# A state-space layer on Trainium2: scratch and powers of VectorE's complex products in PSUM, another layout for the gated unit's inputs, another order on GpSimd

## The chip, the cores and the metric

The kernel runs on one core of a Trainium2 chip. The metric is the device time of one execution in microseconds (us); times shown are medians over runs. The profile is of one such execution.

## The reference

A two-layer decoder trunk on 512 tokens of width 1024, all in float32. Layer 0 mixes tokens with a diagonal complex state-space model (64 groups of 16 channels, 64 states each), then a gated unit, layer norm and a dense SwiGLU block. Layer 1 is latent attention followed by a routed SwiGLU block with 8 experts, of which each token takes 2. The change touches the state-space mixer and what hands its result to the gated unit:

```python
lb_re = mag * jnp.cos(li * dt)
lb_im = mag * jnp.sin(li * dt)
...
bb_re = f_re[..., None] * br - f_im[..., None] * bi
bb_im = f_re[..., None] * bi + f_im[..., None] * br
...
_, _, s_re, s_im = lax.associative_scan(_s5_combine, (a_re, a_im, bu_re, bu_im), axis=0)
y = (jnp.einsum('sbgp,gcp->bsgc', s_re, c_re.astype(f32))
     - jnp.einsum('sbgp,gcp->bsgc', s_im, c_im.astype(f32)))
y = y.reshape(bsz, seq, D_MODEL) + d_skip.astype(f32) * uf
act = jax.nn.gelu(y).astype(u.dtype)
val, gate = jnp.split(act @ w_glu, 2, axis=-1)
return val * jax.nn.sigmoid(gate)
```

## The kernel before

The 512 tokens are cut into 64 blocks of 8 (j is the block, t the token in it). Within a block the recurrence is worked out as matrices, and only the 64 block states are scanned. The 64 groups lie two to a column of 128 partitions (2 groups x 64 states), so there are 32 columns; they are worked on in two halves of 16. All complex tensors have an axis of two, real and imaginary.

For each half `h` there are:

- **A** (`s5_a`, L1829): the input factors of the 8 tokens of a block, 128 x 2 x 16 x 128, made from `bb` by complex products (`cmul`) with powers of the diagonal (`self.pw`, three powers).
- **O** (`s5_o`, L1913): the output factors, made in the same way from C.
- **E** (`s5_e`, L1768): unit phases of the 64 blocks, always made by GpSimd. With them the scan runs on real decays.
- **the input pass** (`s5_in`, L1840): PE transposes A (L1853), ScalarE copies it out of PSUM (L1854), PE multiplies with the tokens U (L1870), and `turn` (L1876) rotates each block of four columns by E into S. A pass has four such turns.
- **the scan** (`s5_scan`, L1887): two VectorE scans (L1893) and four turns back, SBUF to SBUF.
- **K** (`s5_k`, L1947): PE makes the within-block kernels from O and bz; ScalarE copies them out, and 16 small transfers on SP's queue (for half 1, four of them on GpSimd's) write the block-Toeplitz tile T.
- **y** (`s5_y`, L1979): two calls for each half; PE multiplies T with U and O with S, ScalarE applies the gelu.
- **hand-over** (`s5_act`, L2008): for each y, eight PE transposes into two PSUM banks; ScalarE writes the float16 high part (L2018), VectorE subtracts it from the bank for the low part (L2019). Both are written with the token's position in its block as the slow axis, so that neighbours of one instruction lie 8 elements apart.

`cmul` (L1778) does a complex product in three steps: `tensor_mul` of the swapped parts into a scratch tile (L1792), `tensor_mul` by the real part (L1798), `tensor_add` of the scratch (L1799). For long rows on VectorE the last two are one `scalar_tensor_tensor` per column (L1795). The scratch tile is in SBUF, one for VectorE (`s5_ctv`, shared with `turn`) and one for GpSimd (`s5_ctp`). In `turn` L1881 writes the scratch, L1882 the other product, and L1885 twice adds or subtracts the scratch in place:

```python
V.tensor_mul(t, self.swap(x), E[:, 1, None].to_broadcast(sh))
V.tensor_mul(dst, x, E[:, 0, None].to_broadcast(sh))
for part in range(2):
    op = V.tensor_add if back == (part == 0) else V.tensor_sub
    op(dst[:, part], dst[:, part], t[:, part])
```

**What sets the order.** The program is written out by hand and each engine works through its own instructions in the order in which `run` (L2022) issues them. VectorE makes O and A of half 0; GpSimd makes E of both halves and then A of half 1; VectorE does the turns and scans and O of half 1. After scan 0 come the first chunk of the gated unit's weights (`st.load(1)`, `st.convert(1)`: ScalarE L102, then VectorE L103), 36 matmuls that keep PE busy (`warm`, L270), y of half 0, its hand-over, the input pass, K and scan of half 1. Weight chunks are loaded on SP's queue. PSUM is one pool of 8 banks of 128 x 512 floats for everything (`bank`, L250). `glu_quarter` (L294) then does the gated unit in four quarters of the columns. Its first half quarter needs the hand-over of half 0 alone; y and hand-over of half 1 are issued inside the first quarter. After that come the dense block, attention and the experts.

Of the kernel before, what the change touches and what calls it, by code (L numbers as in the profile page):

```python
# [20 lines left out]
L = 8  # L21
# [102 lines left out]
class Kernel:  # L124
    def __init__(self, tc, A, out, dev=None):
        self.tc, self.nc, self.A, self.out = tc, tc.nc, A, out
        self.dev = dev or {}
        self.pools = []

    def pool(self, name, side, **kw):  # L130
# [119 lines left out]
    def bank(self, name="ps"):  # L250
        return self.ps.tile([128, 512], F, name=name, tag="ps", bufs=8)

# [1398 lines left out]
    def s5_params(self):  # L1651
# [73 lines left out]
        for i in range(3):  # L1725
            if i:
                re, im = P[:, i - 1, 0], P[:, i - 1, 2]
                V.tensor_mul(t[:, 0], re, re)
                V.tensor_mul(t[:, 1], im, im)
                V.tensor_sub(P[:, i, 0], t[:, 0], t[:, 1])  # L1730
                V.scalar_tensor_tensor(P[:, i, 2], re, 2.0, im, op0=OP.mult, op1=OP.mult)
            V.tensor_scalar(P[:, i, 1::2], P[:, i, 2, None, :].to_broadcast([128, 2, 32]), -1.0, None, op0=OP.mult)
        self.bb = self.r3.tile([128, 2, 32, GC], F, name="s5_bb")
        self.cmul(V, self.bb, self.b, f, 0, 32)
# [42 lines left out]

    def cmul(self, eng, dst, x, cf, g0, g1, conj=False):  # L1778


        n = x.shape[3]
        step = min(g1 - g0, 512 // n)
        cr = cf[:, 0, None, :, None]
        ci = cf[:, 2:4] if conj else cf[:, 1:3]
        nm = "s5_ctv" if eng is self.nc.vector else "s5_ctp"
        for g in range(g0, g1, step):
            s = slice(g, g + step)
            sh = [128, 2, step, n]
            t = self.r3.tile([128, 2, 512], F, name=nm, tag=nm, bufs=1)[:, :, :step * n]
            t = t.rearrange("p a (g n) -> p a g n", n=n)  # L1790
            xs = x[:, :, s]
            eng.tensor_mul(t, self.swap(xs), ci[:, :, s, None].to_broadcast(sh))  # L1792
            if n >= 64 and eng is self.nc.vector:
                for i in range(step):
                    eng.scalar_tensor_tensor(dst[:, :, g + i], x[:, :, g + i], cf[:, 0, g + i:g + i + 1], t[:, :, i],  # L1795
                                             op0=OP.mult, op1=OP.add)
                continue
            eng.tensor_mul(dst[:, :, s], xs, cr[:, :, s].to_broadcast(sh))  # L1798
            eng.tensor_add(dst[:, :, s], dst[:, :, s], t)  # L1799
# [29 lines left out]
    def s5_a(self, eng, h):  # L1829
        A = self.wp.tile([128, 2, 16, L * GC], F, name="s5_A", tag="wf", bufs=2)  # L1830
        at = lambda t0, t1: A[:, :, :, t0 * GC:t1 * GC]
        hs = slice(h * 16, h * 16 + 16)
        pw = lambda i: self.pw[:, i, :, hs]
        self.cmul(eng, at(7, 8), self.bb[:, :, hs], pw(0), 0, 16)
        self.cmul(eng, at(6, 7), at(7, 8), pw(0), 0, 16)
        self.cmul(eng, at(4, 6), at(6, 8), pw(1), 0, 16)
        self.cmul(eng, at(0, 4), at(4, 8), pw(2), 0, 16)
        return A
# [74 lines left out]
    def s5_o(self, eng, h):  # L1913
        hs = slice(h * 16, h * 16 + 16)
        ot = lambda l0, l1: self.O[:, :, hs, l0 * GC:l1 * GC]
        for i, n in enumerate((1, 2, 4)):
            self.cmul(eng, ot(n, 2 * n), ot(0, n), self.pw[:, i, :, hs], 0, 16, conj=True)

# [89 lines left out]
    def s5_act(self, dp):  # L2008
        nc = self.nc
        y = self.ydt.pop(dp)  # L2010
        for t0 in (0, 4):
            p = self.bank()
            for t in range(4):
                nc.tensor.transpose(p[:, t * 128:(t + 1) * 128], y[:, t0 + t].rearrange("j i q c -> j (i q c)"), self.ident)
            pv = p.rearrange("p (t r j) -> p r t j", t=4, r=2)
            hi, lo = (x[:, 2 * dp:2 * dp + 2].rearrange("p r (j t) -> p r t j", t=L)[:, :, t0:t0 + 4]
                      for x in (self.xh, self.xl))
# [4 lines left out]
    def run(self):  # L2022
# [7 lines left out]
        self.YD = dram.tile([SEQ, D], F, name="YD")  # L2030
        psA = self.ps = self.pool("psA", None, space=bass.MemoryType.PSUM)
        self.wp = self.pool("w", "right")
        self.big = self.pool("big", "left")
        if phases != "moe":
# [13 lines left out]
            self.s5_u()  # L2048
            E = [self.s5_e(nc.gpsimd, h) for h in range(2)]
            self.s5_o(V, 0)  # L2050
# [16 lines left out]
            st.load(1)  # L2067
            st.convert(1)
            self.warm(36)
            self.s5_y(0)  # L2070
# [4 lines left out]
            self.xh, self.xl = Halves(None, None), Halves(None, None)  # L2075
            self.s5_xt(0)
            self.s5_act(0)
            self.s5_act(1)
            self.s5_in(1, A1, E[1])
            del A1  # L2080
            self.s5_k(1)
            self.bz = None
            self.s5_scan(1, E[1])
            E = self.dec = None
            st.load(2)
            self.r3.release()
# [63 lines left out]
        keep()  # L2150
        psA.release()
        self.hp = self.pool("moe_h", "right")
# [53 lines left out]
```

## Time and profile before

| | |
|---|---|
| median of 3 runs | 1884.29 us (1880.74 to 1885.18) |
| the profiled execution | 1883.41 us, of which the span is 1881.6 us |
| mean granted TensorE clock | 0.963 of full speed |
| busy: PE, VectorE (DVE), ScalarE (ACT), GpSimd (POOL) | 1741.5, 1443.9, 1011.5, 237.3 us |
| HBM read, mean rate over the span | 416.81 MB, 228 GB/s |

How to read it: the span runs from the first to the last instruction of the core, and the times in the rows further down count from its start. PE is the matrix engine, PEld its weight loads, SP the queue that issues most transfers. Busy time is the time in which an engine's instructions run, so a VectorE instruction that is held up while it runs counts as busy. [...] What stands in brackets behind a row is the idle time of that engine just before it and what ended it.

### The profile page before, as it was taken

To read this page: it belongs to the slowest core of one execution; us is meant where nothing else is said; L and a number is where in the kernel's file an instruction comes from. 1 tells how busy PE (TensorE), PEld (TensorE's weight loads), DVE (VectorE), ACT (ScalarE), POOL (GpSimd) and SP (SyncE) were. 2 spreads that over 40 slices of the span, in tenths; PEclk is the share of its full clock that TensorE was granted. 3 is DMA by queue.
4 is the path that set the end of the run, shared out by engine and by line. 5 is a ranking of instruction groups with operands and counts; after the bars stand their busy time and mean duration, and the time that the engine had idled before them with its cause. 6 is when DMAs were issued, how large, how long until landed. Compare 5 with 4: busy or idle time off the path is not lost.

```text
span 1881.6 us, 45134 instructions
## 1 busy us (share of the span) xinstructions
PE 1741.5 (93%) x19567; PEld 1371.7 (73%) x19567; DVE 1443.9 (77%) x2048; ACT 1011.5 (54%) x1091; POOL 237.3 (13%) x232
## 2 busy tenths in 40 slices
PE   6578989999999788979999999999999999999984
PEld 5445455444444555569999999999999899999963
DVE  9995473333324877569999999999999899999987
ACT  4233343223222466257776666666766677766772
POOL 6940010000000100200000022120000100000035
PEclk9679999999999899979999999999999999999997
DMA  4105803433323210189999999999999999999991
GB/s 85 45 23 170 236 26 90 112 93 108 111 92 88 79 46 1 45 294 378 372 339 339 347 340 332 339 347 342 367 355 349 302 361 380 361 373 360 359 375 59
DMA packets 359393, 433.79 MB, mean 231 GB/s; under 512 B 30520, under 2 KB 321424, under 8 KB 359184
## 3 DMA queue, kind: packets, MB, share of 16 engines
q1 hardware_dynamic: 346832, 417.55, 65.7%
q0 software_dynamic: 4064, 12.72, 2.4%
q8 instruction: 155, 2.54, 0.6%
q10 hardware_dynamic: 8288, 0.54, 0.3%
q14 instruction: 54, 0.44, 0.1%
HBM read 416.81 MB, written 11.34 MB: 228 GB/s over the span
## 4 chain that ended last, share of the span: by engine, by line
PE 75%; DVE 15%; ACT 3%; issue 3%; DMA 3%; POOL 1%; DVEq 0%; ACTq 0%; POOLq 0%
PE gu L274 10%; PE gu L276 10%; PE gu L275 10%; PE ps L275 6%; PE ps L276 6%; PE ps L274 6%; PE y L274 5%; PE y L275 5%; PE y L276 5%; DVE wi L1095 2%; PE gu L1043 2%; DMA mraw<-in_moe_w_in_dram 2%; PE glu L276 1%; PE glu L274 1%; PE glu L275 1%
## 5 line engine op out<-in xcount | busy, mean ns | idle before, releaser
L276 PE MATMUL gu<-xe,wi 128*128 128x132 f16 (+7 forms) x3584 | 658.8, 225 | 17.7 <-DVE wi L1095 17.7
L274 PE MATMUL gu<-xe,wi 128*128 128x132 f16 (+7 forms) x3584 | 658.8, 225 | 6.3 <-ACT yr L1180 3.4
L275 PE MATMUL gu<-xe,wi 128*128 128x132 f16 (+7 forms) x3584 | 658.8, 224 | 0.0
L1095 DVE SCALAR_TENSOR_TENSOR wi<-mraw,wi 128x2048 f16<-128x2048 f32 x224 | 511.9, 2285 | 13.5 <-ACT wi L1089 13.5
L1089 ACT ACTIVATE wi<-mraw 128x2048 f16<-128x2048 f32 x224 | 420.8, 1904 | 32.3 <-DMA mraw<-in_moe_w_in_dram 29.5
L276 PEld LDWEIGHTS <-wi 128*128 128x128 f16 x3584 | 352.2, 98 | 19.4 <-DVE wi L1095 19.3
L275 PEld LDWEIGHTS <-wi 128*128 128x128 f16 x3584 | 353.4, 99 | 8.5 <-issue 3.8
L274 PEld LDWEIGHTS <-wi 128*128 128x128 f16 x3584 | 352.5, 98 | 6.7 <-ACT wi L1089 3.0
L1095 DVE SCALAR_TENSOR_TENSOR wol<-mraw,woh 128x2048 f16<-128x2048 f32 x112 | 255.8, 2284 | 0.2 <-ACT woh L1089 0.2
L1089 ACT ACTIVATE woh<-mraw 128x2048 f16<-128x2048 f32 x112 | 213.3, 1904 | 7.3 <-DMA mraw<-in_moe_w_out_dram 7.3
L275 PE MATMUL y<-hl,woh 128*128 128x132 f16 (+4 forms) x1120 | 215.9, 227 | 0.0
L276 PE MATMUL y<-hh,wol 128*128 128x132 f16 (+4 forms) x1120 | 215.9, 227 | 0.0
L274 PE MATMUL y<-hh,woh 128*128 128x132 f16 (+4 forms) x1120 | 215.9, 227 | 0.0
L1112 ACT ACTIVATE hs<-gu 128x168 f32<-128x168 f32 (+5 forms) x224 | 63.5, 284 | 270.1 <-PE gu L276 269.8
L103 DVE SCALAR_TENSOR_TENSOR wf<-raw,wf 128x2048 f16<-128x2048 f32 x37 | 84.9, 2297 | 118.4 <-ACT wf L102 118.4
L1147 POOL DMA_INDIRECT XD<-yr,at x12 | 24.8, 2068 | 807.2 <-ACT yr L1180 442.4
L102 ACT ACTIVATE wf<-raw 128x2048 f16<-128x2048 f32 x37 | 70.5, 1909 | 100.7 <-PE ps L276 67.5
L276 PE MATMUL ps<-xt,wf 128*128 128x512 f16 x320 | 121.3, 379 | 0.0
L275 PE MATMUL ps<-xt,wf 128*128 128x512 f16 x320 | 121.3, 379 | 0.0
L274 PE MATMUL ps<-xt,wf 128*128 128x512 f16 x320 | 121.3, 379 | 0.0
L274 PEld LDWEIGHTS <-woh 128*128 128x128 f16 x1120 | 109.6, 98 | 0.0
L275 PEld LDWEIGHTS <-woh 128*128 128x128 f16 x1120 | 109.6, 98 | 0.1
(462 smaller groups left out, 2888.6 us busy)
## 6 DMA issues: line engine op xcount, KB each, us to landing
mraw<-in_moe_w_in_dram SPq DMA_DIRECT2D x224, 1024.0 KB
mraw<-in_moe_w_out_dram SPq DMA_DIRECT2D x112, 1024.0 KB
raw<-in_ffn_w_in_dram SPq DMA_DIRECT2D x44, 512.0 KB
raw<-in_ffn_w_out_dram SPq DMA_DIRECT2D x11, 1024.0 KB
raw<-in_s_w_glu_dram SPq DMA_DIRECT2D x64, 128.0 KB
raw<-in_mla_o_w_dram SPq DMA_DIRECT2D x4, 1024.0 KB
XD<-X SPq DMA_DIRECT2D x5, 512.0 KB
xj<-in_x_dram SPq DMA_DIRECT2D x4, 512.0 KB
```

Source lines behind the costliest of these rows:

```text
L102: nc.scalar.activation(hi[:, c], raw[:, c], AF.Copy, scale=scale[j])
L103: nc.vector.scalar_tensor_tensor(lo[:, c], raw[:, c], scale[j], hi[:, c], op0=OP.mult, op1=OP.subtract)
L274: mm(out, lh, rh, start=first, stop=False, **kw)
L275: mm(out, lh, rl, start=False, stop=False, **kw)
L276: mm(out, ll, rh, start=False, stop=last, **kw)
L1043: nc.tensor.matmul(p[:, (k - k0) * cap:(k - k0 + 1) * cap], x[:, tt, k * 128:(k + 1) * 128], sel[:, tt, :cap], start=tt == 0, stop=tt == T ...
L1089: nc.scalar.activation(hi, raw, AF.Copy, scale=WS)
L1095: self.nc.vector.scalar_tensor_tensor(lo, raw, WS, hi, op0=OP.mult, op1=OP.subtract)
L1112: nc.scalar.activation(sg, p[:, :cap], AF.Silu, scale=1.0 / (WS * XS))
L1147: self.nc.gpsimd.indirect_dma_start(out=self.XD, out_offset=bass.IndirectOffsetOnAxis(ap=self.at[:n, j:j + 1], axis=0), in_=yr[:n], in_off ...
```

## The change

VectorE's scratch tile moves from SBUF to a PSUM pool of its own (`psT`), for `cmul` and for `turn`. ScalarE copies the powers there too (`pwp`), and VectorE's products take them from it; the per-column scalar of L1795 still comes from SBUF. GpSimd's tiles stay in SBUF. While the state-space stage runs, the pool for everything else has 5 banks instead of 8; after scan 1 both pools are released and the old pool of 8 is opened.

GpSimd makes E of half 0, then A of half 1, then E of half 1. The second `warm` goes. The input pass of half 1 moves ahead of the hand-over of half 0, and the conversion of the first weight chunk moves from before y to behind that pass.

The hand-over writes, for each block, four tokens that lie next to each other. For even pairs (`dp`) it reads the transposes from PSUM with the token as the fastest axis, 128 floats apart; for odd pairs PE writes the transposes with a step of 4 floats, and the reads are in order.

```diff
@@ def bank
-        return self.ps.tile([128, 512], F, name=name, tag="ps", bufs=8)
+        return self.ps.tile([128, 512], F, name=name, tag="ps", bufs=self.nps)
@@ def s5_params
+        self.pwp = self.pt.tile([128, 3, 4, 32], F, name="s5_pwp")
+        nc.scalar.activation(self.pwp, P, AF.Copy)
         self.bb = self.r3.tile([128, 2, 32, GC], F, name="s5_bb")
@@ def power, def cmul
+    def power(self, eng, i, h):
+        return (self.pwp if eng is self.nc.vector else self.pw)[:, i, :, h * 16:h * 16 + 16]
...
-            t = self.r3.tile([128, 2, 512], F, name=nm, tag=nm, bufs=1)[:, :, :step * n]
+            if eng is self.nc.vector:
+                t = self.pt.tile([128, 2, 512], F, name=nm, tag=nm, bufs=1)[:, :, :step * n]
+            else:
+                t = self.r3.tile([128, 2, 512], F, name=nm, tag=nm, bufs=1)[:, :, :step * n]
...
-                    eng.scalar_tensor_tensor(dst[:, :, g + i], x[:, :, g + i], cf[:, 0, g + i:g + i + 1], t[:, :, i],
+                    eng.scalar_tensor_tensor(dst[:, :, g + i], x[:, :, g + i], one[:, 0, g + i:g + i + 1], t[:, :, i],
@@ def s5_a (s5_o likewise)
-        self.cmul(eng, at(0, 4), at(4, 8), pw(2), 0, 16)
+        self.cmul(eng, at(0, 4), at(4, 8), pw(2), 0, 16, one=self.pw[:, 2, :, hs])
@@ def turn
-        t = self.r3.tile([128, 2, 4 * NJ], F, name="s5_ctv", tag="s5_ctv", bufs=1)[:, :, :4 * NJ]
+        t = self.pt.tile([128, 2, 512], F, name="s5_ctv", tag="s5_ctv", bufs=1).rearrange(
+            "p a (i n) -> p (a i n)", n=4 * NJ)[:, :8 * NJ]
@@ def s5_act
+            if dp % 2:
+                pt = p.rearrange("p (r j t) -> p t r j", t=4, r=2)
+                pv = p.rearrange("p (r j t) -> p r j t", t=4, r=2)
+            else:
+                pt = p.rearrange("p (t r j) -> p t r j", t=4, r=2)
+                pv = p.rearrange("p (t r j) -> p r j t", t=4, r=2)
             for t in range(4):
-                nc.tensor.transpose(p[:, t * 128:(t + 1) * 128], y[:, t0 + t].rearrange("j i q c -> j (i q c)"), self.ident)
-            pv = p.rearrange("p (t r j) -> p r t j", t=4, r=2)
-            hi, lo = (x[:, 2 * dp:2 * dp + 2].rearrange("p r (j t) -> p r t j", t=L)[:, :, t0:t0 + 4]
+                nc.tensor.transpose(pt[:, t], y[:, t0 + t].rearrange("j i q c -> j (i q c)"), self.ident)
+            hi, lo = (x[:, 2 * dp:2 * dp + 2].rearrange("p r (j t) -> p r j t", t=L)[:, :, :, t0:t0 + 4]
                       for x in (self.xh, self.xl))
@@ def run
-        psA = self.ps = self.pool("psA", None, space=bass.MemoryType.PSUM)
+            self.ps = self.pool("psS", None, space=bass.MemoryType.PSUM)
+            self.nps = 5
+            self.pt = self.pool("psT", None, space=bass.MemoryType.PSUM)
...
-            E = [self.s5_e(nc.gpsimd, h) for h in range(2)]
+            E = [self.s5_e(nc.gpsimd, 0)]
...
             A1 = self.s5_a(nc.gpsimd, 1)
+            E.append(self.s5_e(nc.gpsimd, 1))
...
             st.load(1)
-            st.convert(1)
-            self.warm(36)
             self.s5_y(0)
             self.s5_o(V, 1)
             self.s5_y(1)
...
             self.s5_xt(0)
+            self.s5_in(1, A1, E[1])
+            del A1
+            st.convert(1)
             self.s5_act(0)
             self.s5_act(1)
-            self.s5_in(1, A1, E[1])
-            del A1
             self.s5_k(1)
             self.bz = None
             self.s5_scan(1, E[1])
             E = self.dec = None
+            self.pt.release()
+            self.ps.release()
+            self.nps = 8
+            self.ps = self.pool("psA", None, space=bass.MemoryType.PSUM)
```

## Rows read from the trace of the kernel before

**Rows 1.** Busy us by stretch: each engine (x instructions), PE clock, DMA share, GB/s.

```profile
62.00:78.00 16.00, 14.34 (x120) 11.23 (x116) 15.48 (x18) 8.05 (x8) 15.21 (x16) 0.92 0.03 11
78.00:112.00 34.00, 16.06 (x120) 9.16 (x120) 33.55 (x21) 1.19 (x2) 31.04 (x15) 0.61 0.04 16
...
260.00:1881.00 1621.00, 1541.81 (x18040) 1248.43 (x18038) 1241.64 (x1732) 920.22 (x988) 133.25 (x112) 0.98 0.74 251
```

**Rows 2.** All runs of two lines: ns min/median/max, first and last start.

```profile
L1881 DVE TENSOR_TENSOR s_ctv<-ps,s_E x8: 682/683/841, 62.4 to 141.9; 128x504 f32<-128x504 f32 x8
L1881 DVE TENSOR_TENSOR s_ctv<-s_S,s_E x8: 682/684/2707, 84.4 to 155.0; 128x504 f32<-128x504 f32 x8
...
L1885 DVE TENSOR_TENSOR s_S<-s_S,s_ctv x32: 414/422/2554, 63.7 to 156.8; 128x252 f32<-128x252 f32 x32
```

**Rows 3.** VectorE in order of time, 0 to 420 us: start us, length us, instructions.

```profile
19.86 1.22 DVE L1792 TENSOR_TENSOR s_ctv<-b,s_f 128x1024 f32<-128x1024 f32 x1
...
46.53 6.62 DVE L1795 SCALAR_TENSOR_TENSOR s_A<-s_A,s_pw,s_ctv 128x128 f32<-128x128 f32 x8
...
56.10 6.14 DVE L1795 SCALAR_TENSOR_TENSOR s_A<-s_A,s_pw,s_ctv 128x128 f32<-128x128 f32 x8
...
78.15 6.19 DVE L1893 TENSOR_TENSOR_SCAN s_S<-dec,s_S 128x1024 f32<-128x1024 f32 x2
...
110.77 0.75 DVE L1885 TENSOR_TENSOR s_S<-s_S,s_ctv 128x252 f32<-128x252 f32 x2
...
113.64 0.68 DVE L1792 TENSOR_TENSOR s_ctv<-s_O,s_pw 128x512 f32<-128x512 f32 x1
...
120.60 2.19 DVE L1795 SCALAR_TENSOR_TENSOR s_O<-s_O,s_pw,s_ctv 128x128 f32<-128x128 f32 x8
...
124.08 2.19 DVE L1795 SCALAR_TENSOR_TENSOR s_O<-s_O,s_pw,s_ctv 128x128 f32<-128x128 f32 x8
```

**Rows 4.** ScalarE in order of time, 0 to 260 us.

```profile
11.21 3.10 ACT L1910 ACTIVATE s_O<-ps 64x256 f32<-64x256 f32 x8
...
31.75 1.26 ACT L1940 ACTIVATE s_bz<-s_bb 64x512 f32<-64x512 f32 x2
...
119.93 9.31 ACT L2018 ACTIVATE xt<-ps 128x512 f16<-128x512 f32 x4
```

**Rows 5.** TensorE (PE) in order of time, 95 to 260 us.

```profile
119.18 1.97 PE L2014 MATMUL ps<-ident,s_y 128*128 128x128 f32 x16
...
129.72 1.12 PE L1870 MATMUL ps<-s_U,s_at 128*64 128x64 f32 x16 [7.69 <-ACT s_at L1854]
...
140.03 0.39 PE L1964 MATMUL ps<-s_O,s_bz 128*64 128x128 f32 x4
...
150.61 0.39 PE L274 MATMUL glu<-wf,xt 128*128 128x512 f16 x1
...
181.80 0.61 PE L274 MATMUL glu<-wf,xt 128*128 128x512 f16 x1 [3.50 <-ACT xt L2018]
...
184.26 0.61 PE L276 MATMUL glu<-wf,xt 128*128 128x512 f16 x1 [1.42 <-DVE xt L2019]
```

**Rows 6.** GpSimd in order of time, 0 to 420 us.

```profile
38.57 0.12 POOL L1771 MEMSET s_E<- 128x16 f32 x1
...
60.16 0.13 POOL L1771 MEMSET s_E<- 128x16 f32 x1
...
76.66 1.11 POOL L1792 TENSOR_TENSOR s_ctp<-s_bb,s_pw 128x512 f32<-128x512 f32 x1
...
106.62 2.40 POOL L1799 TENSOR_TENSOR s_A<-s_A,s_ctp 128x1024 f32<-128x1024 f32 x1
```

**Rows 7.** VectorE's L1881 between 78 and 109.3 us: busy us, mean ns.

```profile
L1881 DVE TENSOR_TENSOR s_ctv<-s_S,s_E 128x504 f32<-128x504 f32 x3 | 6.3, 2110 | 0.1
```

**Rows 8.** The lo half of `transpose_tt`, 0 to 420 us: busy us, mean ns.

```profile
L264 DVE TENSOR_TENSOR xt<-ps,xt 128x512 f16<-128x512 f32 x8 | 5.0, 683 | 0.1
```

**Rows 9.** ScalarE: the conversion of the fifth weight chunk.

```profile
206.43 1.91 ACT L102 ACTIVATE wf<-raw 128x2048 f16<-128x2048 f32 x1 [8.18 <-DMA raw<-in_s_w_glu_dram]
```

More of the change, by code (lines that the diff above doesn't have):

```diff
@@ L1776, in s5_e, with cmul @@
         return E
-    def cmul(self, eng, dst, x, cf, g0, g1, conj=False):
+    def power(self, eng, i, h):
+        return (self.pwp if eng is self.nc.vector else self.pw)[:, i, :, h * 16:h * 16 + 16]
+    def cmul(self, eng, dst, x, cf, g0, g1, conj=False, one=None):
         n = x.shape[3]
@@ L1832, in s5_a @@
         hs = slice(h * 16, h * 16 + 16)
-        pw = lambda i: self.pw[:, i, :, hs]
+        pw = lambda i: self.power(eng, i, h)
         self.cmul(eng, at(7, 8), self.bb[:, :, hs], pw(0), 0, 16)
@@ L1878, in turn @@
         sh = list(x.shape)
-        t = self.r3.tile([128, 2, 4 * NJ], F, name="s5_ctv", tag="s5_ctv", bufs=1)[:, :, :4 * NJ]
-        t = t.rearrange("p a (g n) -> p a g n", g=4)[:, :, :, :sh[3]]
+        t = self.pt.tile([128, 2, 512], F, name="s5_ctv", tag="s5_ctv", bufs=1).rearrange(
+            "p a (i n) -> p (a i n)", n=4 * NJ)[:, :8 * NJ]
+        t = t.rearrange("p (a g n) -> p a g n", a=2, g=4)[:, :, :, :sh[3]]
         V.tensor_mul(t, self.swap(x), E[:, 1, None].to_broadcast(sh))
@@ L1916, in s5_o @@
         for i, n in enumerate((1, 2, 4)):
-            self.cmul(eng, ot(n, 2 * n), ot(0, n), self.pw[:, i, :, hs], 0, 16, conj=True)
+            self.cmul(eng, ot(n, 2 * n), ot(0, n), self.power(eng, i, h), 0, 16, conj=True, one=self.pw[:, i, :, hs])
     def s5_dd(self):
@@ L2030, in run @@
         self.YD = dram.tile([SEQ, D], F, name="YD")
-        psA = self.ps = self.pool("psA", None, space=bass.MemoryType.PSUM)
+        if phases != "moe":
+            self.ps = self.pool("psS", None, space=bass.MemoryType.PSUM)
+            self.nps = 5
+            self.pt = self.pool("psT", None, space=bass.MemoryType.PSUM)
+        else:
+            self.ps = self.pool("psA", None, space=bass.MemoryType.PSUM)
         self.wp = self.pool("w", "right")
@@ L2084, in run @@
             E = self.dec = None
+            self.pt.release()
+            self.ps.release()
+            self.nps = 8
+            self.ps = self.pool("psA", None, space=bass.MemoryType.PSUM)
             st.load(2)
@@ L2150, in run @@
         keep()
-        psA.release()
+        self.ps.release()
         self.hp = self.pool("moe_h", "right")
```

## The prediction

> **What bounds the kernel now.** I read the busy times by stretch first [rows 1]. From 260 us on PE is busy 1541.81 of 1621 us, in stages that the change leaves alone and that start when the gated unit has its data: what the state-space stage ends earlier, the end gains, unless a weight transfer is late. So I follow the first 190 us. There VectorE is the engine without gaps: 33.55 of 34 us in 78 to 112, while PE is busy 16.06 at a granted clock of 0.61 and waits for it. GpSimd is nearly as full (31.04).
>
> Next, two lines in all their runs [rows 2]. L1885, two inputs in SBUF, takes 414 ns at least, 422 in the median and 2554 at most. L1881 with both inputs in SBUF spreads likewise (682 to 2707), and with one input in PSUM hardly: 682 to 841 over 8 runs, the first of them at 62.4 us, in a stretch in which GpSimd was busy 15.21 of 16 us [rows 1]. So it is not a busy GpSimd that slows VectorE, but a busy GpSimd beside two SBUF inputs. The order of VectorE's work [rows 3] shows what that costs: eight L1795 take 6.62 and 6.14 us at 46 and 56 us, and 2.19 at 120 us, when GpSimd is done; the two scans take 6.19.
>
> The order of the stage in the kernel before: the A factor of half 0 is done at 62.2, the recurrence's input at 78.1, its scan at 111.5; then 2.1 us of weight conversion and O's second half to 126.3 [rows 3]. ScalarE's 9.31 us of hi copies (L2018) from 119.9 [rows 4] hold the copies that PE's second input pass needs until 129.7; K of half 1 ends and the gated unit begins at 150.6 [rows 5].
>
> **The change part by part.** Times below are on the axis of the profiled execution.
>
> *Scratch and powers in PSUM.* VectorE's L1795, L1799, L1885 and all L1792 and L1798 but those of the first product then have at most one SBUF input; the scans and the turn after them (L1893, L1881 and L1882 on S) still have two. I price the first at their undisturbed rows. A0's tail, 46.53 to 62.24 (15.7 us), becomes the 5.7 us of the same instructions between 120.60 and 126.27 [rows 3]: A0 is done at 52.2. Reading PSUM cost L1881 nothing in the median (683 against 684 ns); a write to it by VectorE has no row, and I bound its price by 0 and by 0.16 us an instruction (L1881's slowest with a PSUM input over its fastest) and take 0, as the reads show. Some 113 instructions on the path get a PSUM operand (2 in the first product, 24 for each half of O, 27 for A0, 12 for each of three rounds of turns), so the upper end is 18 us. [...]
>
> *The copy of the powers.* It stands in ScalarE's queue ahead of L1910, which ran at 11.21, and waits for the powers, ready when the first product starts at 19.86 [rows 3, 4]. With some 0.5 us for it, L1910 starts at 20.5, and all behind it is up to 9.3 us late: U, the zeroing of T, bz (done at 33.0) and with it K of half 0, from 33.0 to 42.3. K takes 10.6 us (140.03 to 150.61 [rows 5]), so PE starts the input pass at 52.9. O's first columns are there at 22.8 (20.5 and six of eight copies in 3.10), before O's first product at about 23.5: no cost. So the pass is held by K and A0 alike. It takes 10.3 us (129.72 to 140.03), 1.4 ahead for the first transposes and their copy and 2.1 for the last turn: done at 67 against 78.1. With five banks instead of eight the next transposes may wait for a turn; I leave 0 to 2 us for that.
>
> *GpSimd's order.* E of half 0 took 21.6 us and E of half 1, with fewer collisions, 16.5 [rows 6]. At 16.5 the first is done at 55, and earlier still if the work ahead of it is undisturbed too; the first turn, at 56, needs it. A1 follows at once, at most the 32.4 us that it took, to 87 at the latest; then E1, to 98 to 104. If E1 gets the place in SBUF that the scan's E gives up last, it starts at 90 and ends at 106.5, 4 us after its first use below; I take no wait and keep the 4 for the range.
>
> *Scan of half 0.* From 67: scans 6.2 as before [rows 3]. A turn is L1881 and L1882 at 2.1 us each beside A1 [rows 7] and a pair of L1885 in 0.75 (at 110.77 [rows 3]) instead of up to 2.55 each: 5.0 beside A1, and 2.1 to 3.5 beside E1's short first products. Two and a half of the one, one and a half of the other: 6.2 + 12.5 + 4.2 = 23, done at 90 against 111.5. With all four turns undisturbed or all at 5.0 it is 82 or 93.
>
> *Moved: conversion, the hi and lo copies, the input pass.* VectorE goes straight to O's second half, 12.6 us (113.64 to 126.27 [rows 3]): 102.6. PE's y ended 7.7 us after the scan (119.2 against 111.5 [rows 3, 5]): 97.7, so the pass has its first bank at 101, and E1 is ready. No conversion (2.1) and no lo copies stand ahead of the turns, four times 2.1: they end at 111.2. Behind them wait the conversion, then the copies, then scan 1; PE does the copies' 16 transposes and K. K must wait for the last turns' banks: 10.6 us from about 112, ending 122.5 instead of 150.6. **Minus 28 us.** T's transfers and the weight chunks behind them on SP's queue follow K as they do now, and shift with it; on GpSimd's queue the y transfers and T's memset stand behind E1, at 104, well ahead of T's at 122. Scan 1 ends near 131, ahead of the y that needs it (122.5 + 10.4 for the gated unit's first half quarter). The second warm-up's 36 matmuls go; PE idled after them, at a clock of 0.61 [rows 1], so that costs nothing.
>
> *Four tokens at a time.* The hi copies take 2.33 us each (9.31 for 4), each writing every eighth half word; L264, the same subtraction with whole runs, takes 683 ns [rows 8]. The new form writes runs of four, but reads PSUM, or has PE write it, at a stride, for which there is no row. Lower end 0.7, upper end twice now, 4.7; I take 1.2, nearer to the row of equal shape. For half 0 these copies are behind the path. For half 1 two hi copies and a lo copy end PE's waits at 181.80 and 184.26 [rows 5]: 3 times 1.1 and a little of PE's clock, **minus 4 us** (from minus 6 to plus 7). More might not arrive: one weight chunk is converted at 206.43 as it lands [rows 9]. [...]
>
> *Sum.* 1883.4 - 28 - 4 = 1851.4 for an execution like the profiled one; the median of the runs shown lies 0.9 above that one, so 1852.
>
> **The rivals.** *A, the wait moves to the PSUM pools.* The eight-bank pool is opened behind the release of the scratch pool, whose last user is scan 1. If the gated unit's first banks wait for its end, about 131, and not only for the banks underneath, it starts 8 us later than K ends: 1860. For it: both releases stand ahead of the new pool in the program. Against: the scratch covers three banks of eight. Chance 0.12.
>
> *B, the change doesn't do what it says:* PSUM operands don't free VectorE, since L1885 and L1799 write where they read and L1795 still takes its scalar from SBUF, and that is enough to collide. Then the scan still ends at 111 and only the removed queueing stays, 9 us of hi and lo copies ahead of the turns, and 4 at the end: 1871. Against it stand the 8 runs of L1881 with one SBUF input and an SBUF output. Chance 0.07.
>
> *C, slower: PSUM operands are dear to VectorE.* Place: the 113 instructions above; the price must pass 32 / 113 = 0.28 us each before the kernel is slower than now; at 0.4 it is 1852 + 45 = 1897. For it: no row has VectorE writing PSUM. Against: the PSUM reads of rows 2. [...] Chance 0.05, and 0.02 for a price near break-even.
>
> **How the numbers follow.** The forecast has 0.74. Its own range: scan 0 from -8 to +3, banks and E1 up to 6, copies -2 to +11 at the far end, PSUM price up to 18, not all at one end: 1843 to 1866. With A inside, and B at its end, I give 1843 to 1871, which leaves out C and the tails. A measurement here can tell 0.3%, 5.7 us, from no change. Faster are the forecast, A and B: 0.93; the same 0.02; slower 0.05.
>
> **What would show it.** L1885 at 0.42 us in every run and eight L1795 in 2.2, with GpSimd busy beside them; E of half 0 done by 55; scan 0 done near 90, K near 122, the gated unit's first matmul right behind it; L2018 and L2019 near 1 us; the stretch behind the gated unit unchanged in length. I am wrong if L1885 keeps its spread (B), if the first matmul waits for VectorE's last turn (A), or if VectorE's undisturbed instructions grow (C).

## The result, and the profile after

The changed kernel takes 1853.3 us (median of 4 runs, 1853.13 to 1857.72), the kernel before beside it 1883.5: a ratio of 0.9847, 95% interval 0.9827 to 0.9866. The forecast was 1852 in a range of 1843 to 1871, so sign, size and range hold. The way there does not hold at every step: one of the two terms came out too small, the other too large. The profiled execution took 1853.13 us with a span of 1851.4, which is 30.2 less than the span before; its mean granted clock is 0.972.

Line numbers move. `cmul` is L1801, L1804 (`scalar_tensor_tensor`), L1807 and L1808; the turn L1891, L1892 and L1895; the scan L1903; the hand-over L2030 on PE, L2033 on ScalarE, L2034 on VectorE; the gated unit's matmuls L275 to L277.

First the collisions. All runs of L1895 and L1891, which were L1885 and L1881 in [rows 2]:

```profile
L1895 DVE TENSOR_TENSOR s_S<-s_S,s_ctv x32: 409/414/418, 56.7 to 125.1; 128x252 f32<-128x252 f32 x32
```

```profile
L1891 DVE TENSOR_TENSOR s_ctv<-ps,s_E x8: 691/692/692, 55.4 to 105.6; 128x504 f32<-128x504 f32 x8
L1891 DVE TENSOR_TENSOR s_ctv<-s_S,s_E x8: 692/734/2207, 72.2 to 123.3; 128x504 f32<-128x504 f32 x8
```

The spread of L1895, 414 to 2554 ns before, is gone: no run is above 418. L1891 keeps its spread only where both inputs are still in SBUF. The eight runs with an input in PSUM have lost even the one of 841 ns; that one, which bounded the price of a PSUM operand in the prediction, stood at 135.22 us, when GpSimd was idle.

VectorE in order of time, to be held against [rows 3]:

```profile
19.93 1.22 DVE L1801 TENSOR_TENSOR s_ctv<-b,s_f 128x1024 f32<-128x1024 f32 x1
...
24.25 0.68 DVE L1807 TENSOR_TENSOR s_O<-s_O,s_pwp 128x512 f32<-128x512 f32 x1
...
45.23 2.16 DVE L1804 SCALAR_TENSOR_TENSOR s_A<-s_A,s_pw,s_ctv 128x128 f32<-128x128 f32 x8
...
48.68 2.16 DVE L1804 SCALAR_TENSOR_TENSOR s_A<-s_A,s_pw,s_ctv 128x128 f32<-128x128 f32 x8
50.82 0.09 DVE L1854 MEMSET s_S<- 128x32 f32 x1
55.35 0.69 DVE L1891 TENSOR_TENSOR s_ctv<-ps,s_E 128x504 f32<-128x504 f32 x1 [4.45 <-PE ps L1879]
...
64.41 7.72 DVE L1903 TENSOR_TENSOR_SCAN s_S<-dec,s_S 128x1024 f32<-128x1024 f32 x2
72.17 2.21 DVE L1891 TENSOR_TENSOR s_ctv<-s_S,s_E 128x504 f32<-128x504 f32 x1
74.41 2.70 DVE L1892 TENSOR_TENSOR s_S<-s_S,s_E 128x504 f32<-128x504 f32 x1
77.14 0.74 DVE L1895 TENSOR_TENSOR s_S<-s_S,s_ctv 128x252 f32<-128x252 f32 x2
...
85.45 0.69 DVE L1801 TENSOR_TENSOR s_ctv<-s_O,s_pwp 128x512 f32<-128x512 f32 x1
...
109.74 2.48 DVE L2034 TENSOR_TENSOR xt<-ps,xt 128x512 f16<-128x512 f32 x4
112.13 4.47 DVE L1903 TENSOR_TENSOR_SCAN s_S<-dec,s_S 128x1024 f32<-128x1024 f32 x2
...
124.75 0.74 DVE L1895 TENSOR_TENSOR s_S<-s_S,s_ctv 128x252 f32<-128x252 f32 x2
```

Eight L1804 take 2.16 us where they took 6.62 and 6.14, so A of half 0 is done at 50.8 instead of 62.2. VectorE then waits 4.45 us for the input pass. Scan 0, its two scans and four turns, runs from 64.4 to 85.4 (78.15 to 111.5 before). What keeps two SBUF inputs is still slow beside GpSimd's last products of A, the scans even slower than before: they take 7.72 (6.19 before), the first turn's products 2.21 and 2.70. Here is GpSimd in order of time:

```profile
31.08 0.12 POOL L1774 MEMSET s_E<- 128x16 f32 x1
...
46.62 1.06 POOL L1801 TENSOR_TENSOR s_ctp<-s_bb,s_pw 128x512 f32<-128x512 f32 x1
...
61.82 1.90 POOL L1807 TENSOR_TENSOR s_A<-s_A,s_pw 128x1024 f32<-128x1024 f32 x1
...
69.95 3.88 POOL L1807 TENSOR_TENSOR s_A<-s_A,s_pw 128x1024 f32<-128x1024 f32 x1
...
76.51 0.12 POOL L1774 MEMSET s_E<- 128x16 f32 x1
...
91.86 2.35 POOL L1808 TENSOR_TENSOR s_E<-s_E,s_ctp 128x1024 f32<-128x1024 f32 x1
```

The same product takes 1.90 us beside VectorE's work on PSUM (61.82) and 3.88 beside the scans and the first turn (69.95): the two engines hold each other up. With [rows 6]: E of half 0 starts at 31.1 instead of 38.6 and ends at 46.6 instead of 60.2; A1 ends at 76.5, E1 at 94.2.

PE and ScalarE where the two stages meet, to be held against [rows 4, 5]. PE in order of time:

```profile
105.32 1.97 PE L2030 MATMUL ps<-ident,s_y 128*128 128x128 f32 x16
107.22 0.44 PE L1974 MATMUL ps<-s_O,s_bz 128*64 128x128 f32 x4
...
117.52 0.39 PE L1982 MATMUL ps<-s_O,s_bz 128*64 128x128 f32 x4
125.64 0.59 PE L275 MATMUL glu<-wf,xt 128*128 128x512 f16 x1 [7.73 <-DVE s_S L1895]
...
137.44 0.44 PE L2003 MATMUL ps<-s_T,s_U 128*64 128x128 f32 x4
...
152.69 1.97 PE L2030 MATMUL ps<-ident,s_y 128*128 128x128 f32 x16
...
155.43 0.39 PE L277 MATMUL glu<-wf,xt 128*128 128x512 f16 x1 [0.23 <-DVE xt L2034]
```

The places of y of half 1 and of its transposes in the kernel before:

```profile
161.07 0.44 PE L1993 MATMUL ps<-s_T,s_U 128*64 128x128 f32 x4
...
176.33 1.97 PE L2014 MATMUL ps<-ident,s_y 128*128 128x128 f32 x16
```

ScalarE in order of time, after:

```profile
20.04 0.50 ACT L1735 ACTIVATE s_pwp<-s_pw 128x384 f32<-128x384 f32 x1 [8.73 <-DVE s_pw L1733]
20.47 3.11 ACT L1920 ACTIVATE s_O<-ps 64x256 f32<-64x256 f32 x8
...
106.50 2.04 ACT L2033 ACTIVATE xt<-ps 128x512 f16<-128x512 f32 x4
...
175.97 1.91 ACT L102 ACTIVATE wf<-raw 128x2048 f16<-128x2048 f32 x1 [8.18 <-DMA raw<-in_s_w_glu_dram]
```

K of half 1 ends near 117.9, 32.8 us earlier than before, but the gated unit does not follow it: its first matmul stands 7.73 us still and is released at 125.64 by L1895, the last turn of scan 1. That is rival A. The hi copies take 2.04 us for four instead of 9.31, and the first matmul of the gated unit's second part that needs a lo copy starts 2.74 us after the start of the transposes (155.43 against 152.69) instead of 7.93 (184.26 against 176.33 in the kernel before).

Busy times by stretch, columns as in [rows 1]:

```profile
78.00:107.00 29.00, 28.56 (x363) 20.21 (x360) 26.96 (x52) 9.40 (x15) 20.30 (x18) 0.90 0.10 38
...
260.00:1851.00 1591.00, 1511.01 (x17821) 1224.35 (x17818) 1225.20 (x1688) 909.26 (x968) 134.82 (x110) 0.98 0.75 255
```

From 78 to 107 PE is now busy throughout (28.56 of 29 us), where it had 16.06 of 34 and waited for VectorE. The rest of the kernel, from 260 us on, is as full as it was: PE is busy 95% of the time here and in [rows 1].

The account of the 30.2 us follows the path. The gated unit starts 25.0 earlier (125.64 against 150.61). Its first half quarter loses 1.3 of that (11.8 us until y of half 1 at 137.44, against 10.5), because PE comes out of the wait at a lower clock (0.50 in its first 2.6 us); y of half 1 is 23.6 ahead (before: 161.07). The hand-over of half 1 adds 5.2, and 1.6 more follow while PE, which no longer stands still for it, stays at full clock (1.00 from the second part's first lo copy to the conversion, against 0.92 before): the conversion at 175.97 is 30.5 ahead of its place in [rows 9], with the same 8.18 us wait for its weights. The first activation of the dense block is 29.2 ahead (243.62 against 272.80), the end 30.2; the differences behind the conversion are not followed further.

### The profile page after: what moved, and what is told of

It is laid out like the page before. It is cut to its first block, busy times and chain, and to the rows that moved or that the text cites. A ratio compares the mean times of both kernels' runs of the same rounds, so it can differ in the third digit from the quotient of the medians.

```text
span 1851.4 us, 45065 instructions
## 1 busy us (share of the span) xinstructions
PE 1718.7 (93%) x19531; PEld 1357.0 (73%) x19531; DVE 1400.5 (76%) x2048; ACT 998.7 (54%) x1092; POOL 225.2 (12%) x232
## 4 chain that ended last, share of the span: by engine, by line
PE 77%; DVE 12%; ACT 3%; DMA 3%; issue 3%; POOL 1%; DVEq 0%; POOLq 0%; ACTq 0%; SPq 0%
PE gu L275 10%; PE gu L277 10%; PE gu L276 10%; PE ps L276 7%; PE ps L277 7%; PE ps L275 6%; PE y L275 5%; PE y L277 5%; PE y L276 5%; DVE wi L1096 2%; PE gu L1044 2%; DMA mraw<-in_moe_w_in_dram 2%; PE glu L275 1%; PE glu L277 1%; PE glu L276 1%
## 5 line engine op out<-in xcount | busy, mean ns | idle before, releaser
L277 PE MATMUL gu<-xe,wi 128*128 128x132 f16 (+7 forms) x3584 | 658.3, 224 | 19.1 <-DVE wi L1096 19.1
L275 PE MATMUL gu<-xe,wi 128*128 128x132 f16 (+7 forms) x3584 | 658.4, 225 | 6.7 <-ACT yr L1181 3.4
L1090 ACT ACTIVATE wi<-mraw 128x2048 f16<-128x2048 f32 x224 | 421.0, 1906 | 28.3 <-DMA mraw<-in_moe_w_in_dram 25.4
L277 PEld LDWEIGHTS <-wi 128*128 128x128 f16 x3584 | 352.0, 98 | 21.0 <-DVE wi L1096 21.0
L275 PEld LDWEIGHTS <-wi 128*128 128x128 f16 x3584 | 352.2, 98 | 7.1 <-ACT wi L1090 3.4
L277 PE MATMUL y<-hh,wol 128*128 128x132 f16 (+4 forms) x1120 | 215.9, 227 | 0.0
L275 PE MATMUL y<-hh,woh 128*128 128x132 f16 (+4 forms) x1120 | 215.9, 227 | 0.0
L102 ACT ACTIVATE wf<-raw 128x2048 f16<-128x2048 f32 x37 | 70.3, 1903 | 102.1 <-PE ps L277 67.5
L275 PE MATMUL ps<-xt,wf 128*128 128x512 f16 x320 | 121.3, 379 | 0.0
L277 PE MATMUL ps<-xt,wf 128*128 128x512 f16 x320 | 121.3, 379 | 0.0
L1114 DVE SCALAR_TENSOR_TENSOR hf<-gu,hs 128x168 f32<-128x168 f32 (+5 forms) x224 | 66.9, 298 | 60.8 <-ACT hs L1113 60.1
L275 PEld LDWEIGHTS <-woh 128*128 128x128 f16 x1120 | 109.6, 98 | 0.0
```

Of the source, the lines that this page charges most:

```text
L102: nc.scalar.activation(hi[:, c], raw[:, c], AF.Copy, scale=scale[j])
L275: mm(out, lh, rh, start=first, stop=False, **kw)
L277: mm(out, ll, rh, start=False, stop=last, **kw)
L1090: nc.scalar.activation(hi, raw, AF.Copy, scale=WS)
L1114: nc.vector.scalar_tensor_tensor(h, p[:, cap:2 * cap], HS / (WS * XS), sg, op0=OP.mult, op1=OP.mult)
```

## The experiments

Three points of the program's time were read in every run and stand in this table: the gated unit's first matmul and the wait that the profile shows just before it, the first matmul of its second part that needs a lo copy, and the first activation of the dense block (ScalarE's `ffn_s`), all in us from the start of the span. The ratio is to the kernel before, run on the same chip beside the kernel (medians of before: 1883.3, 1879.9 and 1881.0 us in the three groups of timed runs), with its 95% interval.

| kernel | first matmul (wait) | second part | dense block | span | median | ratio |
|---|---|---|---|---|---|---|
| before | 150.61 | 184.26 | 272.80 | 1881.6 | 1883.5 | 1 |
| the change | 125.64 (7.73) | 155.43 | 243.62 | 1851.4 | 1853.3 | 0.9847 [0.9827, 0.9866] |
| e4_early_release | 118.46 (0.69) | 146.88 | 234.02 | 1845.9 | 1845.1 | 0.9794 [0.9778, 0.9811] |
| e7_old_queue | 127.21 (5.08) | 157.50 | 245.94 | 1850.8 | 1850.9 | 0.9841 [0.9817, 0.9864] |
| e2_old_handover | 131.23 (14.60) | 167.06 | 255.41 | 1867.5 | 1868.5 | 0.9923 [0.9906, 0.9940] |
| e8_only_handover | 141.29 | 169.67 | 257.20 | 1866.7 | 1869.0 | 0.9932 [0.9916, 0.9949] |
| e1_sbuf_scratch | 141.84 (0.69) | 170.27 | 257.43 | 1863.1 | 1866.2 | 0.9921 [0.9905, 0.9938] |
| e9_only_psum | 135.71 (5.38) | 171.32 | 260.13 | 1868.7 | 1869.3 | 0.9928 [0.9908, 0.9948] |
| e3_old_gpsimd | 126.10 (7.34) | 156.56 | 243.18 | 1849.9 | 1855.1 | 0.9863 [0.9846, 0.9879] |
| e5_vcopy | 122.44 (6.43) | 153.78 | 240.79 | 1851.5 | 1853.4 | 0.9840 [0.9824, 0.9856] |
| e6_both | 116.90 (0.70) | 145.33 | 233.54 | 1838.0 | 1841.1 | 0.9787 [0.9768, 0.9805] |
| e10_swapped_pools | 125.22 (7.73) | 156.47 | 243.73 | 1852.6 | 1854.4 (one run) | |

A check on the yardstick first: span less the dense block's start is 1604.5 to 1612.1 us in these twelve executions, with no order in it (1608.8 before, 1607.8 after, 1604.5 and 1612.1 at the ends, in e6 and e2). So some 4 us either way come from the unedited rest and say nothing of an edit. The dense block's start leaves that out. How well the start itself repeats is not shown, as there is one trace for each kernel; e10 below, which does the same work as the change, differs from it by 0.1 us.

**Is the new wait the pools, and what does it cost?** The scratch of scan 1 goes back to SBUF, and both pools are handed over ahead of that scan. Nothing else changes, so K ends when it did.

```diff
             self.s5_k(1)
-            self.s5_scan(1, E[1])
             self.pt.release()
             self.ps.release()
             self.nps = 8
             self.ps = self.pool("psA", None, space=bass.MemoryType.PSUM)
+            self.s5_scan(1, E[1], self.r3)     # turn() takes its scratch from this pool
```

> Changed kernel, but the turns of scan 1 take an SBUF scratch and both PSUM pools are released, and the pool of eight opened, ahead of scan 1. If the gated unit's first matmul waits for scan 1 only because the scratch pool's last user is scan 1 (rival A; 7.7 us in the changed kernel's trace): it starts right behind K at about 118, and 5 to 9 us go, 1844 to 1848; less than the 7.7 where the weight chunks, whose transfers stay where they are, land too late. If something else holds it (the weight chunk, T): 1852 to 1854, with the idle time under another name.

Measured: 1845.1 us, ratio 0.9794; the interval lies wholly below that of the change. PE in order of time:

```profile
118.46 0.38 PE L275 MATMUL glu<-wf,xt 128*128 128x512 f16 x1 [0.69 <-ACT s_K L1983]
```

The first matmul follows K's copy with 0.69 us between, at full clock (0.38 instead of 0.59 us), 7.2 us earlier; the second part starts 8.6 earlier, the dense block 9.6. So the wait was rival A's: the new pool of eight banks waits for the last user of the scratch pool, which is scan 1, though the gated unit needs nothing of that scan yet. The change gives 8 to 10 us away there (8.2 by the medians, 9.6 at the dense block).

Whether the pool waits as a whole, or only the one bank that the first matmul takes, is told apart by opening the two pools in the other order, so that the scratch lies under other banks:

```diff
-            self.ps = self.pool("psS", None, space=bass.MemoryType.PSUM)
             self.nps = 5
             self.pt = self.pool("psT", None, space=bass.MemoryType.PSUM)
+            self.ps = self.pool("psS", None, space=bass.MemoryType.PSUM)
...
-            self.pt.release()
             self.ps.release()
+            self.pt.release()
```

> The changed kernel with the scratch pool opened ahead of the pool of five banks instead of behind it, so that the scratch lies under other banks of the later pool of eight; what is computed and the order of the work are unchanged. If the later pool waits as a whole for the last user of the pools before it, the gated unit's first matmul waits for L1895 as before, 7 to 8 us, at about 125.6 us, and the span stays within 4 us of 1851. If it waits bank by bank, its first bank must now lie over the scratch (where it does and did not before) or no longer lie there (where it did): then the wait, which is there in the order of the change, means that the first bank lay over the scratch, and with the other order the first matmul follows K's copy at about 118.5 us with less than 1 us of waiting, and the dense block starts some 9 us earlier, near 234.

```profile
125.22 0.58 PE L275 MATMUL glu<-wf,xt 128*128 128x512 f16 x1 [7.73 <-DVE s_S L1895]
```

PE's order of time again: the same 7.73 us. If the pools are laid out in the order in which they are opened (the traces show no bank numbers), a bank that lies over the scratch in one order doesn't in the other. So the wait does not go by the bank underneath: the new pool waits as a whole.

**What is the order of the second half's work worth?** The input pass goes back behind the hand-over of half 0, and the weight conversion and the 36 matmuls go back ahead of y.

```diff
             st.load(1)
+            st.convert(1)
+            self.warm(36)
             self.s5_y(0)
...
-            self.s5_in(1, A1, E[1])
-            del A1
-            st.convert(1)
             self.s5_act(0)
             self.s5_act(1)
+            self.s5_in(1, A1, E[1])
+            del A1
```

> Changed kernel with the old order of the second half: conversion and warm-up ahead of y, hand-over of half 0 ahead of the input pass. VectorE does the same work before the end of scan 1 in another order. If the gated unit's start hangs on the end of scan 1: plus 0 to 2 us, 1853 to 1855, with K later and the wait behind it shorter. If K's time counts, as I priced it: plus 4 to 6, 1857 to 1859.

Measured: 1850.9 us, a little below the range expected, and 0.9841, the same as the change within both intervals. K starts at 111.5 instead of 107.2, but VectorE has the same work ahead of scan 1 in either order and starts it at 113.81 instead of 112.13, and the start of the gated unit hangs on that:

```profile
127.21 0.61 PE L275 MATMUL glu<-wf,xt 128*128 128x512 f16 x1 [5.08 <-DVE s_S L1895]
```

The move brings K forward by 4.3 us, and 1.6 of it reach the gated unit, 2.3 the dense block: too little for these times to show.

**The hand-over, taken back and alone.** First the changed kernel with the old `s5_act`, then the kernel before with the new one.

```diff
@@ e2: the changed kernel (e8 is the kernel before with the reverse of this)
-            if dp % 2: ... else: ...        # pt, pv as in the change
             for t in range(4):
-                nc.tensor.transpose(pt[:, t], ...)
+                nc.tensor.transpose(p[:, t * 128:(t + 1) * 128], ...)
+            pv = p.rearrange("p (t r j) -> p r t j", t=4, r=2)
-            hi, lo = (... "p r (j t) -> p r j t" ... [:, :, :, t0:t0 + 4]
+            hi, lo = (... "p r (j t) -> p r t j" ... [:, :, t0:t0 + 4]
```

> Changed kernel with the old layout of the hand-over. If only the hand-over of half 1 is on the path, as I priced it: plus 5 to 7 us, 1858 to 1860. If the gated unit's start hangs on the end of scan 1, VectorE's low copies of half 0 (6.6 us longer) stand ahead of that scan and count as well: plus 12 to 14, 1865 to 1867.

> The kernel before with nothing but the new layout of the hand-over. In the kernel before the copies of half 0 stand on ScalarE and VectorE ahead of the input pass of half 1, and the gated unit starts behind that pass and K; the copies of half 1 end PE's waits inside the first quarter. If the copies cost 0.6 and 0.68 us as in the changed kernel, four hi copies take 2.4 us instead of 9.3: both halves lie on the path, the first matmul of the gated unit comes 6 to 7 us earlier (about 144), the second part another 6 us, and the time falls by 11 to 14 us, a ratio of 0.9926 to 0.9942. Rival: half 0 is hidden beside the other work ahead of the pass, and only the 6 to 7 us of half 1 are left: ratio 0.9963 to 0.997. Second rival: the layouts were cheap in the changed kernel only because nothing else was running, and here cost 2 us or more: ratio 0.998 or above.

Measured: 0.9923 without it (1868.5 us, somewhat above the larger of the two losses expected), 0.9932 with it alone (within the forecast). In e2 the gated unit's first matmul waits 14.60 us for scan 1, because VectorE's lo copies stand ahead of that scan and follow ScalarE's hi copies. ScalarE and VectorE in order of time:

```profile
105.09 9.38 ACT L2028 ACTIVATE xt<-ps 128x512 f16<-128x512 f32 x4
```

```profile
108.66 9.33 DVE L2029 TENSOR_TENSOR xt<-ps,xt 128x512 f16<-128x512 f32 x4
...
117.61 4.59 DVE L1903 TENSOR_TENSOR_SCAN s_S<-dec,s_S 128x1024 f32<-128x1024 f32 x2
```

Scan 1 starts 5.5 us later than in the change, and the copies of half 1 then hold PE for 3.6 and 1.9 us (3.50 and 1.42 in [rows 5]). In e8 the four hi copies take 2.06 us and the input pass of half 1, which stands behind them on ScalarE, starts at once; PE in order of time:

```profile
121.76 0.69 PE L1870 MATMUL ps<-s_U,s_at 128*64 128x64 f32 x16 [0.51 <-ACT s_at L1854]
```

It was at 129.72, with 7.69 us of waiting [rows 5]. The gated unit starts 9.3 earlier and its second part 14.6 earlier. Both halves' copies lie on the path, before as after; the prediction had called those of half 0 "behind the path". In the change they lie on it only by way of scan 1, to which the pools tie the gated unit; without that tie the old copies were not run.

**PSUM, taken back and alone.** In the changed kernel scratch and powers go back to SBUF (the copy of the powers is still made, but not read); then the kernel before gets nothing but the move to PSUM.

```diff
@@ e1: the changed kernel
     def power(self, eng, i, h):
-        return (self.pwp if eng is self.nc.vector else self.pw)[:, i, :, h * 16:h * 16 + 16]
+        return self.pw[:, i, :, h * 16:h * 16 + 16]
@@ cmul, turn
-                t = self.pt.tile([128, 2, 512], F, ...)
+                t = self.r3.tile([128, 2, 512], F, ...)
@@ e9: the changed kernel with e7's and e2's edits and the old order on GpSimd (as in e3, below)
```

> Changed kernel with VectorE's scratch and powers back in SBUF; order, hand-over and pools as changed (ScalarE still copies the powers, nobody reads the copy). If two SBUF inputs beside a busy GpSimd are what PSUM removes: A0 is done near 62, scan 0 near 103, and though the gated unit then needn't wait for scan 1, it starts 10 to 16 us later: 1863 to 1869, L1895 with a spread to 2.5 us again. If order and hand-over carry the gain: below 1857.

> Kernel before with the scratch and powers in PSUM and the pools of 5 and 3 banks alone; old order on GpSimd and in the second half, old hand-over. If the collisions are the larger part: scan 0 ends near 92 instead of 111.5, the wait for scan 1 takes 7 to 8 back: minus 11 to 16 against before, 1867 to 1873. If they aren't: above 1876.

Measured: 0.9921 without PSUM, 0.9928 with it alone. All runs of L1895 in e1:

```profile
L1895 DVE TENSOR_TENSOR s_S<-s_S,s_ctv x32: 413/422/2553, 69.0 to 148.5; 128x252 f32<-128x252 f32 x32
```

The spread of [rows 2] is back to within a nanosecond, and with it A of half 0 at 67.5 and scan 0 from 84.9. In e9, with every other part of the change undone but the pools and the copy of the powers, no L1895 is above 418 ns and scan 0 starts at 64.8. So where the two inputs lie decides, and nothing else in the change; scratch and powers were not moved one by one. And e1 does not wait for scan 1 (0.69, behind K's copy), although that scan ends later than the gated unit starts there, at 141.84. VectorE in order of time:

```profile
148.17 0.75 DVE L1895 TENSOR_TENSOR s_S<-s_S,s_ctv 128x252 f32<-128x252 f32 x2
```

With the scratch in SBUF scan 1 uses nothing of the PSUM pools. That is rival A once more, seen from the other side.

The two halves of the gain add up. The hand-over alone brings the dense block 15.6 us forward, PSUM alone 12.7; the sum is 28.3, and the whole change brings 29.2. That they add up so well is partly chance: PSUM alone pays 5.38 us for the pools, which the hand-over alone does not, and taken back one at a time out of the change they lose 11.8 and 13.8, which is 25.6.

**GpSimd's order.** E of both halves first, then A1.

```diff
-            E = [self.s5_e(nc.gpsimd, 0)]
+            E = [self.s5_e(nc.gpsimd, h) for h in range(2)]
...
             A1 = self.s5_a(nc.gpsimd, 1)
-            E.append(self.s5_e(nc.gpsimd, 1))
```

> Changed kernel with GpSimd's old order, E of both halves before A1. If the short products of E beside the scan are worth it: scan 0 runs all its turns beside A1's long products, at 4.5 to 5 us a turn instead of 2.4, and ends 6 to 9 us later; 1859 to 1862. If the order doesn't matter (A1 is ready in time either way): 1853.

Measured: 1855.1 us, ratio 0.9863; the interval overlaps that of the change. The four times (1851.7 to 1856.6) lie below the loss expected, 1859 to 1862, but the kernel before ran 3.6 us faster in this group too, so by the ratio the low end of that loss stays possible, and the trace has to decide. VectorE in order of time:

```profile
64.11 5.49 DVE L1903 TENSOR_TENSOR_SCAN s_S<-dec,s_S 128x1024 f32<-128x1024 f32 x2
...
82.26 1.50 DVE L1891 TENSOR_TENSOR s_ctv<-s_S,s_E 128x504 f32<-128x504 f32 x1
83.79 2.26 DVE L1892 TENSOR_TENSOR s_S<-s_S,s_E 128x504 f32<-128x504 f32 x1
86.08 0.74 DVE L1895 TENSOR_TENSOR s_S<-s_S,s_ctv 128x252 f32<-128x252 f32 x2
```

All four turns are now dear, 3.5 to 5.0 us each, but the scans, which lie beside A1's short products, are 2.2 us cheaper: scan 0 ends at 86.9 instead of 85.4. My expectation had taken all turns of the change for cheap, though its first takes 5.7 us, and had not counted the cheaper scans. A1 ends at 94.5, and the pass, which starts at 90.5 on A1's first columns, shows no wait for it. The new order is worth 1.4 us at the scan and nothing at the dense block (243.18 against 243.62).

**The copy of the powers.** VectorE makes it instead of ScalarE.

```diff
-            nc.scalar.activation(self.pwp, P, AF.Copy)
+            V.tensor_copy(self.pwp, P)
```

> Changed kernel, but VectorE copies the powers to PSUM, so ScalarE isn't held from 11 to 20 us. K of half 0 moves ahead by some 8 us and the input pass can start when A is ready, near 49 instead of 52; VectorE has 0.4 us more. If K holds the pass: minus 1 to 2.5 us, 1851 to 1852. If the scan beside GpSimd's A1, which stays where it is, takes it back: within 0.7 of 1853.

Measured: 0.9840, no difference that these runs can tell. In the trace the 4.45 us that VectorE waits for the first pass are gone:

```profile
51.44 0.69 DVE L1891 TENSOR_TENSOR s_ctv<-ps,s_E 128x504 f32<-128x504 f32 x1
```

Scan 0 starts 4.4 us earlier (60.05), the gated unit 3.2, the dense block 2.8. A gain of that size lies within what the rest of the kernel varies by, and I leave open how much of it reaches the end. So ScalarE's copy does cost something at the front: K of half 0 stands on PE ahead of the input pass. K of half 1 now waits for the bank of its input pass's last turn (L1892 reads it). Here that costs nothing, as the gated unit waits for scan 1 longer; in e6 below, where K has the same 1.59 us of waiting and the gated unit follows it, it counts. PE in order of time:

```profile
103.79 0.44 PE L1974 MATMUL ps<-s_O,s_bz 128*64 128x128 f32 x4 [1.59 <-DVE s_S L1892]
```

**Both remedies together**, e4's and e5's edits:

> Both edits, the early release and VectorE's copy of the powers: the sum of the two, 1842 to 1848, if neither hides the other; as the early release alone if the copy gives nothing or the weight chunks now set the end.

Measured: 1841.1 us, 0.9 below the range expected, ratio 0.9787, the lowest of all. It is faster than both kernels; against e4 the intervals overlap. Of the 1.6 us that the second edit brings here at the first matmul (116.90 against 118.46) 0.5 are left at the dense block, so that the two gains add up is not shown.

```profile
116.90 0.38 PE L275 MATMUL glu<-wf,xt 128*128 128x512 f16 x1 [0.70 <-ACT s_K L1983]
```

## Why the prediction was right, and where it was not

The time was met within 2 us, with the gain at the two places where it was put, and what PSUM operands do was foreseen. That the total fits so closely is partly luck. The term of minus 28 came out as minus 23.6 and that of minus 4 as minus 6.8 at the conversion: errors of 4.4 and 2.8 in opposite directions.

*Scratch and powers in PSUM: right.* A0 was done at 50.8 (predicted 52.2), since the work ahead of it was undisturbed too. The price of a PSUM operand, taken as 0 between 0 and 0.16 us, was some 0.01 for a write (L1891 692 ns into PSUM, 683 into SBUF in [rows 2]; for 1024 elements 1.22 us as in [rows 3]) and nothing for a read (0.68 for 512, as in [rows 3]). L1892 agrees: it takes 0.67 us with its source in PSUM (55.95 us) and 0.68 undisturbed with it in SBUF (119.59). And it was the scratch in PSUM that kept GpSimd's work from slowing L1895: its slowest run takes 2553 ns in e1, with the scratch in SBUF, and 418 in e9 and in the change, with it in PSUM.

*The copy of the powers: right in time, too lenient in its price.* L1920 started at 20.47 (20.5 predicted) and K of half 0 ended at 52.0 (52.9). "The pass is held by K and A0 alike" was wrong: K alone held it. With K out of the way in e5, PE transposes A's first columns from 46.20 on, while VectorE is still at the last ones, and the first turn follows A0 at 51.44; in the change VectorE stands 4.45 us. The pass itself was 1.5 us shorter than the 13.8 I gave it, from 52.0 to 64.3.

*GpSimd's order: the times were early, the reason was not needed.* E0, A1 and E1 ended at 46.6, 76.5 and 94.2 (predicted by 55, by 87 and by 98 to 104). E3 shows that the order is worth 1.4 us; what made scan 0 early is PSUM.

*Scan of half 0: two terms mis-sized, in opposite directions.* Scans 7.7 instead of 6.2, turns 13.3 instead of 16.7. The scans have two SBUF inputs, so a row from the kernel before was no constant: they took 4.47 undisturbed, and 5.5 to 8.1 in the runs here, by what GpSimd did beside them. Scan 0 was done at 85.4 instead of 90.

*Moved: this step failed.* The gated unit did not begin behind K but behind scan 1, at 125.64, which is rival A, to which I gave 0.12; the prediction's own sign of being wrong, a first matmul that waits for VectorE's last turn, is there. The rival's mechanism was worked out correctly, its price too (8 us; 7.2 at the first matmul in e4), and the argument against it, that the scratch covers three banks of eight, is what fell: the new pool waits as a whole (e10). K was done at 117.9 instead of 122.5, for scan 0 was done 4.6 us earlier than predicted; the wait took that and 3.1 more. So the term of minus 28 became minus 25, and minus 23.6 with the lower clock behind the wait. "K must wait for the last turns' banks" was right but came to nothing here: the bank was free at 106.84, when the last L1892 ended, and PE was at its transposes until K began at 107.22. In e5, where these are done sooner, K does wait for it, 1.59 us. Of the 28 us, 21.5 were scan 0's; the rest I put down to moving work. e7 moves it back and loses 4.3 us at K and 1.6 at the gated unit: the shorter copies of half 0 shorten that queue without any move, in e8 by 9.3 us at the gated unit.

*Four tokens at a time: mis-sized.* I took 1.2 us a copy, between 0.7 and 4.7; measured are 2.04 us for four hi copies and 0.68 for a lo copy, the lower end. The term of minus 4 became minus 5.2, and minus 1.6 from PE's clock. All terms together are minus 30.5 at the conversion (30.2 at the end of the span) where the sum had minus 32.

Rivals B and C are excluded by e1 and e9, and by the rows of VectorE after.

## What to carry to other kernels

When two engines slow each other, look in all runs of one line for what separates the slow ones from the fast (here, one input in PSUM); that told the size of the gain before anything was built, and it held in the new kernel. When a pool is closed and another opened over it, ask who uses the old one last: here that user ended the wait of what came after, though that needed nothing of it; give that last user other scratch, or hand over ahead of it. And of several edits that each bring work forward, here only those ahead of the last releaser counted: price them together at that releaser, not each by itself.

## What the runs showed of the hardware that I had not expected

The layout of the new hand-over costs next to nothing on all three engines. PE writes transposes at a step of 4 floats in half of the banks, and 16 of them take 1.97 us as before; from their start to that of PE's next instruction it is 1.90 us (105.32 to 107.22), against 1.81 before (119.18 to 120.99). The copies read floats 512 bytes apart in the other half, and take as long as those that read in order: all eight on ScalarE lie between 583 and 620 ns, all eight on VectorE between 681 and 692. Both lines after, as groups with busy us, mean ns and the idle time before them:

```profile
L2034 DVE TENSOR_TENSOR xt<-ps,xt 128x512 f16<-128x512 f32 x8 | 5.0, 684 | 12.1 <-ACT xt L2033 12.1
...
L2033 ACT ACTIVATE xt<-ps 128x512 f16<-128x512 f32 x8 | 4.1, 601 | 0.0
```

Their means were 2700 and 2534 ns before; 684 is what [rows 8] show for whole runs. On ScalarE what cost the fourfold was the write of single half words 16 bytes apart, for the old copies read PSUM in order too, 64 floats at a time; VectorE both reads the high part and writes the low part at that step, and the runs do not separate the two.

The second surprise is what 7.7 us of waiting leave behind. The windows around the wait, columns as in [rows 1]:

```profile
118.00:125.60 7.60, 0.00 (x0) 0.00 (x0) 7.15 (x15) 0.56 (x1) 2.31 (x4) 0.74 0.66 151
125.60:128.20 2.60, 2.56 (x7) 0.91 (x8) 0.00 (x0) 0.00 (x0) 0.00 (x0) 0.50 0.35 63
128.20:137.00 8.80, 8.80 (x42) 4.01 (x41) 0.00 (x0) 0.00 (x0) 0.00 (x0) 0.99 0.61 205
```

PE was fully busy until 117.9, idle for 7.7 us, and then ran its first matmuls at a granted clock of 0.50, one every 0.43 us instead of 0.216, before it was back at 0.99. That is the 1.3 us lost in the first half quarter, and in the kernel before the same happened behind the two waits of the second part, of 3.50 and 1.42 us [rows 5]: the clock is 0.50 from 181.7 to 183.0 and from 184.2 to 185.6. So these waits on PE cost a little more than their length, but not each did: in e2 the two matmuls behind the wait of 3.56 us took 0.39 and 0.38 us, as at full clock.
